# Rotary columns of the latent queries: one matrix product for both, the sine and cosine products taken from one copy

## The chip, the cores and the metric

The kernel runs on one core of one Trainium2 chip. The metric is the device time of one execution in microseconds (us); the figure for a kernel is the median of its runs. TensorE (PE) multiplies matrices, VectorE (DVE), ScalarE (ACT) and GpSimd (POOL) work on elements, and SyncE (SP) issues most of the DMAs. SBUF is the working memory of 128 partitions; PSUM takes the results of TensorE in banks of 128 x 512 floats.

## The reference, cut to what matters

A stack of two layers of a first block and one layer of a second runs over 256 tokens of 1024 features in fp32. Each of the two layers has a mixer, in which half of the heads use latent attention. Eight heads have queries of 96 features: 64 are used as they are ("nope") and 32 are rotated by the token's position. The rotated key is shared by the heads.

```python
def rope(x, positions):
    half = x.shape[-1] // 2
    ...
    x1 = x[..., :half].astype(jnp.float32)
    x2 = x[..., half:].astype(jnp.float32)
    out = jnp.concatenate([x1 * cos - x2 * sin, x2 * cos + x1 * sin], axis=-1)
...
q = (rms_norm(c_q, q_norm_g) @ w_uq).reshape(B, S, MLA_HEADS, MLA_QK_DIM)
q = jnp.concatenate([q[..., :MLA_NOPE_DIM], rope(q[..., MLA_NOPE_DIM:], positions)], axis=-1)
kv = (rms_norm(c_kv, kv_norm_g) @ w_ukv).reshape(B, S, MLA_HEADS, MLA_NOPE_DIM + MLA_V_DIM)
k_pe = rope(k_rope[:, :, None, :], positions)
k = jnp.concatenate([k_nope, k_pe], axis=-1)
o_mla = causal_block_attention(q, k, v_mla).reshape(B, S, MLA_WIDTH)
```

## The kernel before, in words

Every fp32 product is made of three TensorE matmuls (`mm3`, lines 181 to 183): weights and activations are each split into a high part and a low part (ScalarE rounds, VectorE subtracts), and high x high, high x low and low x high are added up in PSUM. The split weights lie in a ring of eight tiles `whl`, fed from a ring of four tiles `raw` that SP's DMAs fill. VectorE, ScalarE and GpSimd instructions that go through the wrappers `V`, `A` and `G` (line 134 in the profile) are given priority over the rest; apart from that, each engine has its instructions in the order that a scheduler wrote when the program was built, and works them off in that order.

`mixer` runs once per layer. It projects the tokens, normalises the latents into `cT` (transposed: features on partitions, tokens along the row), builds the rotated key in `krs`, and then runs the groups of dilated attention and after them the groups of latent attention. At the first latent group the hook `latent()` is called. It loads and splits `w_uq` and `w_ukv`, and projects:

- queries: `w_uq` has 96 columns a head. The split is stored at 128 columns a head: the 96, and after them a copy of the 32 rotary columns with their halves exchanged (the casts of lines 728 and 729). So a head fills 128 partitions of the result: 64 nope, 32 rotary, 32 rotary exchanged. Two heads go into one PSUM bank, four banks in all, one after the other in the same bank `pf1`: 18 matmuls of 256 columns each (`projB`, three k-steps, two column tiles, three matmuls). One VectorE multiplication per bank by the table `Mq` (the scale, the cosines, and the sines with their sign) empties it into `qT`.
- keys: `kT` has 128 partitions a head: 64 nope, the rotated key, and the rotated key a second time. The product of `qT` and `kT` over 128 partitions then adds the cosine part and the sine part of the rotated query.
- two banks for the nope keys and two for the values, through `pf1` too.

While a bank is emptied, TensorE does other work: transposes of the last dilated group (`tp`), and matmuls of a hook that prepares the memory's keys and values for the cross attention (`pf` from `mem_hi` and `mem_lo`); these are called fill here. After the key banks the scores (line 416, `ps` from `kT` and `qT`) begin.

`tables()` computes the angles and `Mq` in layer 0. `b2` and `ones1` belong to the second block, far later (lines 1208 and 1234).

Of the kernel before, what the change touches and what calls it, by code (L numbers as in the profile page):

```python
# [83 lines left out]
def body(nc, tc, I, out, ctx):  # L84
# [61 lines left out]
    trib = const.tile([128, 128], BF16, name="trib")  # L146
    gT1 = const.tile([128, 74], F32, name="gT1")
    gT2 = const.tile([128, 90], F32, name="gT2")
    ones1 = const.tile([1, 128], F32, name="ones1")
    small = const.tile([128, 64], F32, name="small")  # L150
    gatep = [small[:, 0:48].rearrange("p (t h b) -> p t h b", t=2, h=8)]
    rq2 = small[:, 48:64].rearrange("p (t h) -> p t h", t=2)
# [308 lines left out]
    A.activation(junk[:, 0:1], mhalf[:, 0:1], AF.Square)  # L461
    for c in range(2):
        nc.sync.dma_start(x[0][:, c * 512:c * 512 + 512], I["x"][0, 0:128, c * 512:c * 512 + 512])
    G.memset(ones1, 1.0)
    b = ps([128, 16], "pf0")
    PE.transpose(b, g0, ident[:16, :16])
    V.tensor_copy(gT1[:, 0:16], b)
# [98 lines left out]
        scale_heads(dst, src.rearrange("p (h d) -> p h d", h=nh), r, nh, hd)  # L566


    Mq = const.tile([128, T], F32, name="Mq")
    ktab = const.tile([128, 2, 64], F32, name="ktab")  # L570
    f_d = drp.tile([8, 384], F32, name="f_d")

    def tables():
        tb = sc([128, D], True)
        ta = sc([128, D], True)
        rb, oh, fs = tb[0:33, 0:8], tb[0:33, 8:392], tb[0:8, 400:784]
        G.memset(rb, 1.0)
        nc.scalar.dma_start(rb[0:32], I["rel_bias"])
        nc.scalar.dma_start(oh, I["c_bucket"])
        b = ps([8, 384], "tp")  # L580
        PE.matmul(b, rb, oh, start=True, stop=True)
        V.tensor_copy(fs, b)
        nc.scalar.dma_start(f_d, fs)
        pi, a, k = ta[:, 0:T].bitcast(I32), ta[:, T:2 * T], ta[:, 2 * T:3 * T]
        M = ta[:, 3 * T:4 * T]
        nc.scalar.dma_start(pi, I["positions"][0].partition_broadcast(128))
        V.tensor_copy(a, pi)
        V.tensor_scalar(a, a, cm[:, ROPE:ROPE + 1], None, ALU.mult)
        V.tensor_scalar(k, a, 1.0 / TWO_PI, cm[:, ROPE + 1:ROPE + 2], ALU.mult, ALU.add)
        V.tensor_scalar(k, k, MAGIC, None, ALU.add)  # L590
        V.tensor_scalar(k, k, -MAGIC, None, ALU.add)
        for c in (C1, C2, C3):
            V.scalar_tensor_tensor(a, k, -c, a, ALU.mult, ALU.add)
        V.tensor_scalar(a, a, cm[:, ROPE + 2:ROPE + 3], None, ALU.add)
        V.tensor_scalar(a, a, PI_LO, -PI_LO, ALU.min, ALU.max)
        A.activation(M, a, AF.Sin)
        V.tensor_scalar(M, M, cm[:, ROPE + 3:ROPE + 4], None, ALU.mult)
        V.tensor_scalar(Mq, M, 96.0 ** -0.5, None, ALU.mult)
        V.memset(Mq[0:64], 96.0 ** -0.5)

        def rows():
            b = ps([128, 2, 128], "tp")
            for t in range(2):
                PE.transpose(b[:, t], M[:, t * 128:t * 128 + 128], ident)
            V.tensor_copy(ktab, b[:, :, 64:128])

        return rows
# [15 lines left out]
    def mixer(l, hT, first, mid=None, hooks={}):  # L623
# [54 lines left out]
        for t in range(2):  # L678
            kr = krs[:, t]
            p1, p2 = kr[:, 128:160], kr[:, 160:192]  # L680
            V.tensor_tensor(out=p1, in0=kraw[:, t], in1=ktab[:, t, 0:32], op=ALU.mult)
            V.tensor_tensor(out=p2[:, 0:16], in0=kraw[:, t, 16:32], in1=ktab[:, t, 32:48], op=ALU.mult)
            V.tensor_tensor(out=p2[:, 16:32], in0=kraw[:, t, 0:16], in1=ktab[:, t, 48:64], op=ALU.mult)
            G.memset(kr[:, 0:64], 0.0)
            V.tensor_tensor(out=kr[:, 64:96], in0=p1, in1=p2, op=ALU.add)
            V.tensor_tensor(out=kr[:, 96:128], in0=p1, in1=p2, op=ALU.add)
        wd = load_all(w, 8, 1184, 512, gp)
        for i, b in enumerate(projB(wd, hT, 4, "ps", at={6: lambda: memory([0])} if l == 0 else {})):
            copy_any(qkd[:, 1, 2 * i:2 * i + 2], b)
# [25 lines left out]

        def latent():

            wq = []
            for k in range(3):
                raw = rawp.tile([128, 8, 96], F32, tag="raw", name="raw")  # L720
                nc.sync.dma_start(raw, I["w_uq"][l][k * 128:k * 128 + 128, :].rearrange("p (h c) -> p h c", h=8))
                hl = whlp.tile([128, 2, 8, 128], F32R, tag="whl", name="whl")
                g = GI["q_norm_g", l][k]
                nc.scalar.activation(hl[:, 0, :, 0:96], raw, AF.Copy, scale=g)
                nc.vector.scalar_tensor_tensor(hl[:, 1, :, 0:96], raw, g, hl[:, 0, :, 0:96].bitcast(F32), ALU.mult, ALU.subtract)
                for i in range(2):
                    f32v = hl[:, i].bitcast(F32)
                    nc.vector.tensor_copy(hl[:, i, :, 96:112], f32v[:, :, 80:96])
                    nc.vector.tensor_copy(hl[:, i, :, 112:128], f32v[:, :, 64:80])
                wq.append((hl[:, 0].rearrange("p h c -> p (h c)"), hl[:, 1].rearrange("p h c -> p (h c)")))  # L730
            wkv = []
            for k in range(2):
                raw = rawp.tile([128, 8, 128], F32, tag="raw", name="raw")
                nc.sync.dma_start(raw, I["w_ukv"][l][k * 128:k * 128 + 128, :].rearrange("p (h c) -> p h c", h=8))
                hl = whlp.tile([128, 2, 2, 8, 64], F32R, tag="whl", name="whl")
                g = GI["kv_norm_g", l][k]
                for j in range(2):
                    nc.scalar.activation(hl[:, 0, j], raw[:, :, j * 64:j * 64 + 64], AF.Copy, scale=g)
                    nc.vector.scalar_tensor_tensor(hl[:, 1, j], raw[:, :, j * 64:j * 64 + 64], g, hl[:, 0, j].bitcast(F32),
                                           ALU.mult, ALU.subtract)  # L740
                wkv.append([[hl[:, i, j].rearrange("p h c -> p (h c)") for i in range(2)] for j in range(2)])
            qT = s8([128, 8, T], F32, "qT")
            for i in range(4):
                b, = projB([(h_[:, i * 256:], l_[:, i * 256:]) for h_, l_ in wq], cT, 2, "pf1")
                V.tensor_tensor(out=qT[:, 2 * i:2 * i + 2], in0=b, in1=Mq.unsqueeze(1).to_broadcast([128, 2, T]),
                                op=ALU.mult)
            for i in range(2):
                b, = projB([(w_[0][0][:, i * 256:], w_[0][1][:, i * 256:]) for w_ in wkv], cT, 2, "pf1", k0=3)
                for c in range(2):
                    h = 2 * (2 * i + c)  # L750
                    copy_any(kT[0:64, h], b[0:64, c])
                    copy_any(kT[0:64, h + 1], b[64:128, c])
            cTv = (cT[0][:, 3:5], cT[1][:, 3:5])
            for t in range(2):
                b, = projA([w_[1] for w_ in wkv], cTv, t, [(0, 512)], "pf1")
                copy_any(VV[:, t, 0:512], b)
            mla["qT"] = qT
# [241 lines left out]
    def mixer2(hT, first):  # L999
# [92 lines left out]
            V.tensor_tensor(out=v, in0=v, in1=lng[:, 512:], op=ALU.add)  # L1092
        ww = load_all(w, 8, 2048, 280, gp)
        nc.sync.dma_start(w2, I["cmp_w2_2"][0].rearrange("a (k p) d -> p a k d", p=128))
        b2 = smp.tile([1, 128], F32, tag="b2", name="b2", bufs=1)
        nc.sync.dma_start(b2, I["cmp_b2_2"][0:1].rearrange("o a d -> o (a d)"))
        sw = sc([128, 8, 128], True)
        nc.sync.dma_start(sw, I["sg_w_2"][0].rearrange("g t s -> t g s"))
# [328 lines left out]
```

## Time and profile before

| | us |
|---|---|
| median of 3 runs (1206.07 to 1213.22) | 1208.72 |
| the profiled execution | 1211.78 |
| its span, first to last instruction | 1210.0 |
| TensorE busy | 1185.9 (98%) |
| VectorE busy | 780.6 (65%) |
| ScalarE busy | 706.6 (58%) |
| GpSimd busy | 83.9 (7%) |

Busy time is the union of the instructions' spans on an engine. Matmuls overlap in their pipeline, so a busy TensorE can still hold short waits; the distance between the starts of two matmuls tells what one costs. The start of layer 0 up to about 80 us is fed by DMA; the latent projection of layer 0 lies at 111 to 139 us, that of layer 1 at 516 to 544 us. TensorE's mean granted clock is 0.996 of its full 2.4 GHz.

### The profile page before, as it was taken

The numbers are of one execution on the slowest core, as the hardware profiler recorded it, in microseconds if no ns is written. First come the engines' busy times: TensorE is split into PE (matmuls) and PEld (weight loads), VectorE is DVE, ScalarE is ACT, GpSimd is POOL, SyncE is SP. The second block draws the span as 40 slices with busy tenths as digits, with TensorE's granted clock in tenths as the row PEclk, the third lists the DMA queues.
The fourth block names the chain that finished last, engine by engine and source line by source line (L and its number), as shares of the span: only waits on it lengthen the run. The fifth ranks groups of instructions, "written<-read, shape, count | busy, mean of one in ns | idle before, by whom it ended". The sixth has DMA issues, their size and how long they took to land.

```text
span 1210.0 us, 19379 instructions
## 1 busy us (share of the span) xinstructions
PE 1185.9 (98%) x7262; PEld 1029.7 (85%) x7262; DVE 780.6 (65%) x1484; ACT 706.6 (58%) x1434; POOL 83.9 (7%) x161
## 2 busy tenths in 40 slices
PE   8999999999999999999999999999999999999998
PEld 6898888889989899888888889997877787899897
DVE  6767766575565575766757665556767657656653
ACT  7765655565554575745647555556575557645541
POOL 0100010110000020000202000001022011000000
PEclk9999999999999999999999999999998999999999
DMA  8955356266656376543725756655663224665550
GB/s 261 312 181 175 96 201 245 65 229 193 187 180 195 112 263 201 163 138 123 278 88 192 238 179 200 186 178 172 194 210 105 87 88 141 209 190 191 181 187 35
DMA packets 92189, 213.23 MB, mean 176 GB/s; under 512 B 7285, under 2 KB 21055, under 8 KB 91327
## 3 DMA queue, kind: packets, MB, share of 16 engines
q1 hardware_dynamic: 91666, 211.62, 53.8%
q8 instruction: 57, 0.93, 0.3%
q10 hardware_dynamic: 428, 0.37, 0.1%
q14 instruction: 38, 0.30, 0.1%
HBM read 205.66 MB, written 6.30 MB: 175 GB/s over the span
## 4 chain that ended last, share of the span: by engine, by line
PE 77%; DMA 7%; DVE 6%; ACT 6%; issue 2%; POOL 2%; SPq 0%; ACTq 0%; POOLq 0%; DVEq 0%
PE ps L183 11%; PE ps L181 11%; PE ps L182 11%; PE pf L181 8%; PE pf L182 8%; PE pf L183 8%; PE tp L183 3%; PE tp L182 3%; PE tp L181 3%; ACT whl L173 3%; DVE whl L174 2%; PE ps L426 2%; ACT junk L134 1%; PE ps L416 1%; PE ps L827 1%
## 5 line engine op out<-in xcount | busy, mean ns | idle before, releaser
L174 DVE SCALAR_TENSOR_TENSOR whl<-raw,gT,whl 128x512 fp32r<-128x512 f32 (+5 forms) x432 | 307.6, 751 | 117.1 <-ACT whl L173 116.6
L173 ACT ACTIVATE whl<-raw,gT 128x512 fp32r<-128x512 f32 (+5 forms) x432 | 289.3, 717 | 137.6 <-issue 56.0
L170 DVE TENSOR_TENSOR whl<-raw,whl 128x512 fp32r<-128x512 f32 x264 | 170.4, 687 | 92.1 <-ACT whl L169 91.7
L169 ACT ACTIVATE whl<-raw 128x512 fp32r<-128x512 f32 x264 | 152.5, 629 | 108.0 <-issue 86.0
L181 PE MATMUL ps<-whl,mid 128*128 128x512 f32 x384 | 150.2, 391 | 0.0
L182 PE MATMUL ps<-whl,mid 128*128 128x512 f32 x384 | 149.6, 390 | 0.0
L183 PE MATMUL ps<-whl,mid 128*128 128x512 f32 x384 | 149.4, 389 | 0.0
L181 PE MATMUL pf<-hT,whl 128*128 128x256 f32 x352 | 100.0, 284 | 0.0
L182 PE MATMUL pf<-hT,whl 128*128 128x256 f32 x352 | 99.7, 283 | 0.0
L183 PE MATMUL pf<-hT,whl 128*128 128x256 f32 x352 | 99.7, 283 | 0.0
L181 PE MATMUL ps<-whl,hT 128*128 128x512 f32 (+4 forms) x240 | 85.6, 357 | 0.0
L183 PEld LDWEIGHTS ps<-whl,mid 128*128 128x128 f32 x384 | 72.1, 188 | 15.2
L183 PE MATMUL ps<-whl,hT 128*128 128x512 f32 (+4 forms) x240 | 84.1, 350 | 0.4 <-DVE hT L134 0.4
L181 PEld LDWEIGHTS ps<-whl,mid 128*128 128x128 f32 x384 | 72.2, 188 | 14.3
L182 PEld LDWEIGHTS ps<-whl,mid 128*128 128x128 f32 x384 | 72.2, 188 | 14.2
L182 PE MATMUL ps<-whl,hT 128*128 128x512 f32 (+4 forms) x240 | 84.1, 350 | 0.0
L183 PE MATMUL tp<-hT,whl 128*128 128x256 f32 x288 | 81.5, 283 | 0.0
L182 PE MATMUL tp<-hT,whl 128*128 128x256 f32 x288 | 81.5, 283 | 0.0
L181 PE MATMUL tp<-hT,whl 128*128 128x256 f32 x288 | 81.5, 283 | 0.0
L182 PEld LDWEIGHTS pf<-hT,whl 128*128 128x128 f32 x352 | 67.5, 192 | 0.3
L181 PEld LDWEIGHTS pf<-hT,whl 128*128 128x128 f32 x352 | 67.5, 192 | 0.3
L183 PEld LDWEIGHTS pf<-hT,whl 128*128 128x128 f32 x352 | 67.5, 192 | 0.0
(322 smaller groups left out, 2502.2 us busy)
## 6 DMA issues: line engine op xcount, KB each, us to landing
raw<-in_w_up_dram SPq DMA_DIRECT2D x64, 512.0 KB
raw<-in_w_down_dram SPq DMA_DIRECT2D x64, 512.0 KB
raw<-in_w_ff_dram SPq DMA_DIRECT2D x64, 512.0 KB
raw<-in_w_in_dram SPq DMA_DIRECT2D x40, 512.0 KB
raw<-in_w_xk_dram SPq DMA_DIRECT2D x16, 512.0 KB
raw<-in_w_xv_dram SPq DMA_DIRECT2D x16, 512.0 KB
raw<-in_w_mix_out_dram SPq DMA_DIRECT2D x16, 512.0 KB
raw<-in_w_xq_dram SPq DMA_DIRECT2D x16, 512.0 KB
```

Source lines behind the costliest of these rows:

```text
L134: return f(*args, **kw)
L169: nc.scalar.activation(hl[:, 0, c:d], raw[:, c:d], AF.Copy)
L170: nc.vector.tensor_tensor(out=hl[:, 1, c:d], in0=raw[:, c:d], in1=hl[:, 0, c:d].bitcast(F32), op=ALU.subtract)
L173: nc.scalar.activation(hi[:, i], r[:, i], AF.Copy, scale=g[i])
L174: nc.vector.scalar_tensor_tensor(lo[:, i], r[:, i], g[i], hi[:, i].bitcast(F32), ALU.mult, ALU.subtract)
L181: PE.matmul(o, sh, mh, start=start, stop=False, skip_group_check=True)
L182: PE.matmul(o, sh, ml, start=False, stop=False, skip_group_check=True)
L183: PE.matmul(o, sl, mh, start=False, stop=stop, skip_group_check=True)
L416: PE.matmul(s[:, i], qf(h[i], tq), kf(h[i], nk), start=i == 0 and bias is not None, stop=True, skip_group_check=True)
L426: PE.matmul(cell["o"][j * 64:j * 64 + 64, h // 2], vf(h, kb), pp[j][i][kb] if bias is None else pp[j][i][kb][:, ::-1], start=begin and i = ...
L827: PE.matmul(s[:, i], qT[:, c, tq], kT[:, c], start=(i == 0 and k == 0), stop=k == nkt - 1, skip_group_check=True)
```

## The change

The rotary columns are multiplied once. The split of `w_uq` is stored as 256 rotary columns (8 heads x 32) followed by 512 nope columns, without copies, so that the queries need six column tiles in three banks. The first bank holds the rotary columns of all heads, four heads in a column tile. ScalarE copies it to SBUF (`rope`), and from the copy VectorE makes the four products with the cosines (into partitions 64 to 95 of `qT`) and GpSimd the four with the sines (into 96 to 127). The two nope banks are emptied in halves, one by ScalarE and one by VectorE. The exchange of halves moves to the key: its second copy is built exchanged. The table `Mq` becomes `csq`, with the 32 rows of cosines and sines repeated for the four groups of partitions. For space, `b2` and `ones1` now lie in `csq` and `ktab`, and are filled once these are no longer read.

```diff
@@ tables
-        V.tensor_scalar(Mq, M, 96.0 ** -0.5, None, ALU.mult)
-        V.memset(Mq[0:64], 96.0 ** -0.5)
+        for g in range(4):
+            nc.vector.tensor_scalar(csq[32 * g:32 * g + 32, 0], M[64:96], 96.0 ** -0.5, None, ALU.mult)
+            nc.scalar.activation(csq[32 * g:32 * g + 32, 1], M[96:128], AF.Copy, scale=-(96.0 ** -0.5))
@@ mixer, the rotated key
-            V.tensor_tensor(out=kr[:, 96:128], in0=p1, in1=p2, op=ALU.add)
+            V.tensor_tensor(out=kr[:, 96:112], in0=p1[:, 16:32], in1=p2[:, 16:32], op=ALU.add)
+            V.tensor_tensor(out=kr[:, 112:128], in0=p1[:, 0:16], in1=p2[:, 0:16], op=ALU.add)
@@ latent, the split of w_uq
-                hl = whlp.tile([128, 2, 8, 128], F32R, tag="whl", name="whl")
+                hl = whlp.tile([128, 2, 768], F32R, tag="whl", name="whl")
                 g = GI["q_norm_g", l][k]
-                nc.scalar.activation(hl[:, 0, :, 0:96], raw, AF.Copy, scale=g)
-                nc.vector.scalar_tensor_tensor(hl[:, 1, :, 0:96], raw, g, hl[:, 0, :, 0:96].bitcast(F32), ALU.mult, ALU.subtract)
-                for i in range(2):
-                    f32v = hl[:, i].bitcast(F32)
-                    nc.vector.tensor_copy(hl[:, i, :, 96:112], f32v[:, :, 80:96])
-                    nc.vector.tensor_copy(hl[:, i, :, 112:128], f32v[:, :, 64:80])
...
+                for c0, n, o in ((64, 32, 0), (0, 64, 256)):
+                    hi, lo = (hl[:, i, o:o + 8 * n].rearrange("p (h c) -> p h c", h=8) for i in range(2))
+                    nc.scalar.activation(hi, raw[:, :, c0:c0 + n], AF.Copy, scale=g)
+                    nc.vector.scalar_tensor_tensor(lo, raw[:, :, c0:c0 + n], g, hi.bitcast(F32), ALU.mult, ALU.subtract)
@@ latent, the query banks
-            for i in range(4):
+            for i in range(3):
                 b, = projB([(h_[:, i * 256:], l_[:, i * 256:]) for h_, l_ in wq], cT, 2, "pf1")
-                V.tensor_tensor(out=qT[:, 2 * i:2 * i + 2], in0=b, in1=Mq.unsqueeze(1).to_broadcast([128, 2, T]),
-                                op=ALU.mult)
+                if i == 0:
+                    rope = sc([128, 2, T])
+                    A.activation(rope, b, AF.Copy)
+                    for g in range(4):
+                        pr = slice(32 * g, 32 * g + 32)
+                        for j, eng in enumerate((V, G)):
+                            eng.tensor_tensor(out=qT[64 + 32 * j:96 + 32 * j, g:8:4], in0=rope[pr],
+                                              in1=csq[pr, j].unsqueeze(1).to_broadcast([32, 2, T]), op=ALU.mult)
+                else:
+                    h = 4 * (i - 1)
+                    A.activation(qT[0:64, h:h + 4:2], b[0:64], AF.Copy, scale=96.0 ** -0.5)
+                    V.tensor_scalar(qT[0:64, h + 1:h + 4:2], b[64:128], 96.0 ** -0.5, None, ALU.mult)
@@ the second block
-        b2 = smp.tile([1, 128], F32, tag="b2", name="b2", bufs=1)
+        b2 = csq[0:1, 0, 0:128]
+        ones1 = ktab[0:1].rearrange("p t c -> p (t c)")
+        G.memset(ones1, 1.0)
         nc.sync.dma_start(b2, I["cmp_b2_2"][0:1].rearrange("o a d -> o (a d)"))
```

The first place where the order of instructions moves is VectorE in `latent()` of layer 0; `pf` with a number is one query or key bank, `e` are probabilities of the last dilated groups. Before:

```order
L134 TENSOR_TENSOR qT<-pf_1379,Mq 128x512 [waits PE_49]
L134 TENSOR_SCALAR e<-e,den 128x256 [waits DVE_49]
L134 TENSOR_SCALAR e<-e,den 128x256
L134 TENSOR_TENSOR qT<-pf_1399,Mq 128x512 [waits PE_49]
L134 TENSOR_TENSOR qT<-pf_1419,Mq 128x512 [waits PE_49]
L174 SCALAR_TENSOR_TENSOR whl<-raw,gT_95,whl 128x512 [waits DMAHW5_49,Activation_49]
L174 SCALAR_TENSOR_TENSOR whl<-raw,gT_95,whl 128x512 [waits Activation_49]
L134 TENSOR_TENSOR qT<-pf_1439,Mq 128x512 [waits PE_49]
```

and with the change:

```order
L134 TENSOR_SCALAR e<-e,den 128x256 [waits DVE_49]
L134 TENSOR_SCALAR e<-e,den 128x256
L134 TENSOR_TENSOR qT<-sc,csq 32x2x256 [waits Activation_49]
L134 TENSOR_TENSOR qT<-sc,csq 32x2x256 x3
L134 TENSOR_SCALAR qT<-pf_1408 64x2x256 [waits Activation_49]
L173 SCALAR_TENSOR_TENSOR whl<-raw,gT_95,whl 128x512 [waits DMAHW4_49,Activation_49]
L173 SCALAR_TENSOR_TENSOR whl<-raw,gT_95,whl 128x512 [waits Activation_49]
L169 TENSOR_TENSOR whl<-raw,whl 128x512 [waits DMAHW5_49,Activation_49]
L134 TENSOR_SCALAR qT<-pf_1429 64x2x256 [waits Activation_49]
```

VectorE's half of the second bank (`pf_1408`) now stands behind the four cosine products and waits for ScalarE's half. On GpSimd the four sine products stand alone, with nothing near them.

The second place is TensorE at the first scores of layer 0. Before:

```order
L416 MATMUL ps<-kT,qT 128x128 [waits Activation_49]
L416 MATMUL ps<-kT,qT 128x256
L416 MATMUL ps<-kT,qT 128x128 [waits DVE_49]
L182 MATMUL pf_1724<-whl,mem_hi 128x512
L416 MATMUL ps<-kT,qT 128x128 [waits Activation_49]
```

and with the change (lines of helpers are one lower):

```order
L415 MATMUL ps<-kT,qT 128x128 [waits Activation_49,Pool_49]
L415 MATMUL ps<-kT,qT 128x256
L415 MATMUL ps<-kT,qT 128x128 [waits DVE_49,Pool_49]
L415 MATMUL ps<-kT,qT 128x128 [waits Activation_49]
L415 MATMUL ps<-kT,qT 128x256
```

The scores wait for GpSimd now. Ahead of them stand 16 fill matmuls between the banks, as before, and 18 query matmuls fewer.

The third place is SP's queue in the start of layer 0, where the loads of the last weights of the first projection (`w_in`), of the bias table (`H`, through `f_d`), of the memory and of its key weights (`w_xk`) follow each other. Before:

```order
L163 DMA raw_697<-in_w_in_dram 128x2x512 [waits DMAHW4_49,DMAHW2_49,DVE_49]
L614 DMA H_511<-f_d_130 128x8x256 [waits DMAHW1_49]
L163 DMA raw_835<-in_w_xk_dram 128x2x512 [waits DMAHW5_49,DVE_49]
L163 DMA raw_842<-in_w_xk_dram 128x2x512 [waits DMAHW6_49,DVE_49,Activation_49]
L489 DMA sc_641<-in_mem_dram 128x1024 [waits PE_49]
L700 DMA b_d_131<-H_511 128x2048 [waits DMAHW7_49,DMAHW3_49]
L489 DMA sc_652<-in_mem_dram 128x1024 [waits DMAHW0_49,PE_49]
```

and with the change:

```order
L614 DMA H_515<-f_d_128 128x8x256 [waits DMAHW7_49]
L162 DMA raw_703<-in_w_in_dram 128x2x512 [waits DMAHW3_49,DVE_49]
L162 DMA raw_841<-in_w_xk_dram 128x2x512 [waits DMAHW4_49,DVE_49]
L487 DMA sc_645<-in_mem_dram 128x1024 [waits PE_49]
L701 DMA b_d_129<-H_515 128x2048 [waits DMAHW5_49,DMAHW1_49]
L162 DMA raw_848<-in_w_xk_dram 128x2x512 [waits DMAHW6_49,DVE_49,Activation_49]
L487 DMA sc_656<-in_mem_dram 128x1024 [waits PE_49]
```

The bias table goes ahead of the last weights, and the second load of key weights goes behind the first half of the memory and the store `b_d`.

## Rows read from the trace of the kernel before

**Rows 1.** The page: span, and busy time of each engine
```profile
span 1210.0 us, 19379 instructions
...
PE 1185.9 (98%) x7262; PEld 1029.7 (85%) x7262; DVE 780.6 (65%) x1484; ACT 706.6 (58%) x1434; POOL 83.9 (7%) x161
```

**Rows 2.** Timeline of TensorE, layer 0: start us, us, what
```profile
116.24 0.39 PE L181 MATMUL pf<-cT,whl 128*128 128x256 f32 x1
...
119.50 0.31 PE L181 MATMUL pf<-cT,whl 128*128 128x256 f32 x1
...
122.63 0.38 PE L181 MATMUL pf<-cT,whl 128*128 128x256 f32 x1
...
124.88 0.39 PE L181 MATMUL pf<-whl,mem_hi 128*128 128x512 f32 x1
...
128.70 1.12 PE L416 MATMUL ps<-kT,qT 128*128 128x128 f32 x6
```

**Rows 3.** The same timeline, layer 1: first matmul of the fourth bank, and what follows
```profile
527.75 0.38 PE L181 MATMUL pf<-cT,whl 128*128 128x256 f32 x1
...
530.00 0.39 PE L181 MATMUL pf<-whl,mem_hi 128*128 128x512 f32 x1
```

**Rows 4.** Waits, 111 to 135 us: us in total, times, longest
```profile
PEld pf L181 <- DVE qT L134: 0.7, 3, 0.3
```

**Rows 5.** Groups of VectorE by shape, whole run: busy us, mean ns | idle before
```profile
L134 DVE TENSOR_TENSOR qT<-pf,Mq 128x512 f32<-128x512 f32 x8 | 5.5, 691 | 9.4 <-PE pf L183 9.4
...
L729 DVE CAST whl<-whl 128x128 fp32r<-128x128 f32 x12 | 2.7, 224 | 0.0
```

**Rows 6.** Groups of ScalarE by shape, whole run
```profile
L134 ACT ACTIVATE kT<-pf 64x256 f32<-64x256 f32 x8 | 3.0, 378 | 9.7 <-PE pf L183 7.2 <-DVE kT L134 2.4
...
L134 ACT ACTIVATE VV<-pf 128x512 f32<-128x512 f32 x4 | 2.4, 594 | 0.3 <-PE pf L183 0.3
...
L134 ACT ACTIVATE scf<-scf 128x256 f32<-128x256 f32 x1 | 0.4, 417 | 0.0
```

**Rows 7.** Timeline of VectorE, layer 0
```profile
115.49 0.69 DVE L134 TENSOR_TENSOR qT<-pf,Mq 128x512 f32<-128x512 f32 x1 [0.21 <-PE pf L183]
...
124.40 1.41 DVE L174 SCALAR_TENSOR_TENSOR whl<-raw,gT,whl 128x512 fp32r<-128x512 f32 x2 [1.82 <-ACT whl L173]
...
126.33 2.49 DVE L170 TENSOR_TENSOR whl<-raw,whl 128x512 fp32r<-128x512 f32 x4
```

**Rows 8.** Groups of GpSimd by shape, whole run
```profile
L134 POOL TENSOR_TENSOR small<-small,mhalf 128x8 f32<-128x8 f32 x2 | 3.3, 1638 | 0.2
...
L134 POOL TENSOR_TENSOR lv<-lv 128x4 f32<-128x4 f32 x2 | 0.4, 200 | 0.2
```

**Rows 9.** Timeline of VectorE and GpSimd, 245 to 249 us
```profile
245.45 2.07 DVE L174 SCALAR_TENSOR_TENSOR whl<-raw,gT,whl 128x512 fp32r<-128x512 f32 x3
247.44 0.69 DVE L134 TENSOR_TENSOR relu<-relu 128x512 f32<-128x512 f32 x1
...
246.35 1.86 POOL L134 TENSOR_SCALAR lv<-sm 128x1 f32<-128x1 f32 x1 [2.93 <-ACT junk L134]
```

**Rows 10.** Timeline of VectorE and GpSimd, 757 to 760 us
```profile
758.28 2.32 DVE L174 SCALAR_TENSOR_TENSOR whl<-raw,gT,whl 128x512 fp32r<-128x512 f32 x2 [1.04 <-ACT whl L173]
...
758.30 1.10 POOL L134 TENSOR_SCALAR_AFFINE_SELECT scf<-scf 128x1024 f32<-128x1024 f32 x1 [95.30 <-DMA scf<-in_sg_w_dram]
```

**Rows 11.** Windows: stretch, length, busy of PE, PEld, DVE, ACT, POOL, clock, DMA
```profile
140.00:150.00 10.00, 10.00 (x75) 8.14 (x75) 10.00 (x26) 8.70 (x27) 0.00 (x0) 1.00 0.33 105
```

**Rows 12.** Start of layer 0: timeline of ScalarE and TensorE
```profile
50.68 2.73 ACT L173 ACTIVATE whl<-raw,gT 128x512 fp32r<-128x512 f32 x4 [4.04 <-DMA raw<-in_w_xk_dram]
...
54.67 0.44 PE L604 MATMUL tp<-cm,scf 128*128 128x128 f32 x2 [1.69 <-DVE cT L134]
```

**Rows 13.** Start of layer 0: the chain that ended last
```profile
49.77 7.30 DMA sc<-in_mem_dram
```

**Rows 14.** Timeline of SP's queue, layer 1, 530 to 532 us
```profile
530.96 0.33 SPq L163 DMA_DIRECT2D raw<-in_w_mix_out_dram  x1
```

More of the change, by code (lines that the diff above doesn't have):

```diff
@@ L148, in body @@
     gT2 = const.tile([128, 90], F32, name="gT2")
-    ones1 = const.tile([1, 128], F32, name="ones1")
     small = const.tile([128, 64], F32, name="small")
@@ L463, in body @@
         nc.sync.dma_start(x[0][:, c * 512:c * 512 + 512], I["x"][0, 0:128, c * 512:c * 512 + 512])
-    G.memset(ones1, 1.0)
     b = ps([128, 16], "pf0")
@@ L566, in head_norm @@
         scale_heads(dst, src.rearrange("p (h d) -> p h d", h=nh), r, nh, hd)
-    Mq = const.tile([128, T], F32, name="Mq")
+    csq = const.tile([128, 2, T], F32, name="csq")
     ktab = const.tile([128, 2, 64], F32, name="ktab")
@@ L721, in latent @@
                 nc.sync.dma_start(raw, I["w_uq"][l][k * 128:k * 128 + 128, :].rearrange("p (h c) -> p h c", h=8))
-                hl = whlp.tile([128, 2, 8, 128], F32R, tag="whl", name="whl")
+                hl = whlp.tile([128, 2, 768], F32R, tag="whl", name="whl")
                 g = GI["q_norm_g", l][k]
-                nc.scalar.activation(hl[:, 0, :, 0:96], raw, AF.Copy, scale=g)
-                nc.vector.scalar_tensor_tensor(hl[:, 1, :, 0:96], raw, g, hl[:, 0, :, 0:96].bitcast(F32), ALU.mult, ALU.subtract)
-                for i in range(2):
-                    f32v = hl[:, i].bitcast(F32)
-                    nc.vector.tensor_copy(hl[:, i, :, 96:112], f32v[:, :, 80:96])
-                    nc.vector.tensor_copy(hl[:, i, :, 112:128], f32v[:, :, 64:80])
-                wq.append((hl[:, 0].rearrange("p h c -> p (h c)"), hl[:, 1].rearrange("p h c -> p (h c)")))
+                for c0, n, o in ((64, 32, 0), (0, 64, 256)):
+                    hi, lo = (hl[:, i, o:o + 8 * n].rearrange("p (h c) -> p h c", h=8) for i in range(2))
+                    nc.scalar.activation(hi, raw[:, :, c0:c0 + n], AF.Copy, scale=g)
+                    nc.vector.scalar_tensor_tensor(lo, raw[:, :, c0:c0 + n], g, hi.bitcast(F32), ALU.mult, ALU.subtract)
+                wq.append((hl[:, 0], hl[:, 1]))
             wkv = []
```

## The prediction

> **What bounds the kernel.** I read the page first: TensorE is busy for 1185.9 of 1210.0 us, VectorE for 780.6 [rows 1]. That makes TensorE the suspect, but busy spans overlap, so the timeline of the stretch has to say what a matmul costs and whether it waits. In layer 0 the four query banks, the two key banks and the fill between them follow each other from 116.24 to 128.70 us [rows 2], where the scores begin. The waits of this stretch come next: TensorE stood still for VectorE's emptying of a query bank for 0.7 us over three turns [rows 4]. So the stretch is TensorE's own work with small waits, and work taken out of it should be time gained, unless a turn between two banks gets longer. After it, in 140 to 150 us, VectorE is busy all 10 us and ScalarE 8.70 [rows 11]; there the softmax of the latent groups is near a second limit, which has to be weighed below.
>
> **What is removed.** The fourth query bank: 18 matmuls a layer. Its first matmul starts at 122.63 and the fill behind it at 124.88 [rows 2], so it costs 2.25 us; in layer 1 527.75 to 530.00, 2.25 us too [rows 3]. Two layers: 4.50 us. This is exact as far as TensorE goes. The casts of the exchanged columns (24 in all, some 0.22 us each [rows 5]) and the `Mq` products go from VectorE; as TensorE does not wait for them beyond the 0.7 us, I count nothing for them.
>
> **What is added, bank by bank** (layer 0, clock of the trace before).
>
> First bank, complete when VectorE starts on it at 115.49 [rows 7]. VectorE needed 0.69 us, TensorE restarted at 116.24. ScalarE's copy of such a bank takes 0.59 us [rows 6] and ScalarE has nothing else then, so the copy ends at about 116.1 and the second bank can start as before. Two of the four transposes that covered this turn now stand behind the second bank, so I allow 0.1 us.
>
> Second bank: 116.2 plus 2.2 gives 118.4. It is emptied in two halves, VectorE's waiting for ScalarE's. A half has all 512 columns on 64 partitions. The rows bound it from below by the 256-column copy on 64 partitions, 0.38 us, and from above by the whole bank, 0.59 us on ScalarE [rows 6] and 0.69 us on VectorE [rows 5]; the cost goes with columns (0.38 to 0.59 from 256 to 512), so I take 0.59 and 0.69, 1.3 us in turn, and with the handover the bank is free at 119.8. TensorE meanwhile has other work: before, from 116.24 plus 2.25, 118.49, to the third bank at 119.50 [rows 2], 1.0 us of four transposes, a mask matmul and two fill matmuls; now two transposes and one fill matmul more. A query matmul of 256 columns costs 2.25 / 18 = 0.125 us, so by columns these are an estimate of 0.25 and twice 0.06 us. It comes to the third bank at 119.8. No wait, or 0.1 us, if VectorE is free at 119.1. It has the four cosine products first. Four products with two SBUF inputs and 512 columns took 2.49 us back to back [rows 7]: 116.1 to 118.6. Free in time, with half a microsecond to spare.
>
> GpSimd makes the four sine products, and no row shows such an operation there. Below: the 128x1024 select with one input took 1.10 us [rows 10], so 512 columns cannot be much under 0.55 us. Above: twice that for the second input and as much again, 2.2 us. A multiplication of four columns takes 0.20 us, against 1.64 us for a power over eight [rows 8]: multiplications are not in the class of the power. I take 1.1 us, the two-input reading of the select, 4.4 us for four. A sentence from the Trainium skill, page GPSIMD Engine Reference, section 3.1, on an addition of 2048 columns at 4497 ns: a quarter is an estimate of 1.12 us, and the sum would be the same.
>
> **Do the two collide?** Rows 9 and 10 show they can. A one-column GpSimd instruction that takes 0.2 to 0.3 us when undisturbed stood from 246.35 to 248.21, until just after VectorE's run of three weight splits and a square had ended at 248.13 [rows 9]: GpSimd got no turn between four VectorE instructions. The other way round, two weight splits took 2.32 us beside the 1.10 us select [rows 10], where two take 1.41 us [rows 7]: VectorE stood for 0.9 us. The rule behind it is in the Trainium skill, page SBUF, section Who interferes with whom: a VectorE instruction with two SBUF inputs and a GpSimd instruction that reads SBUF take a port pair from each other for a whole instruction, and who issues first decides. Both rows agree with it, and it speaks against this change, which starts both kinds of product on the same event. With VectorE first, as rows 9 suggest for a run, VectorE is not delayed, and GpSimd runs from 118.6 to 123.0. With one GpSimd product first, VectorE is done at 119.7, its half at 120.4, and TensorE waits for 0.5 us. I take 0.15 us a layer.
>
> Third bank: its halves come behind two or three weight splits on either engine. Ten fill matmuls of 512 columns, an estimate of 2.5 us, cover them; two splits of 1.41 us together [rows 7], a third, and VectorE's half (0.69) sum to 2.7, so 0.1 us a layer, between 0 and 0.5.
>
> Scores: they began at 128.70, now at about 126.5. All sine products are there at 123.0: 3.5 us of cover. If that cover is gone, each product costs its own length.
>
> The softmax behind it: VectorE has full use in 140 to 150 us [rows 11], but its work there starts with the scores, and these come earlier by as much, so the gain passes through.
>
> Other edits. The weight split in two pieces costs a start more per k-step and engine: 0.59 less twice the 0.21 us between 0.59 and 0.38 [rows 6] is 0.17 us, three times a layer, beside fill; without cover 0.5 us a layer on either engine, less than the casts that VectorE loses there. `csq` costs four ScalarE instructions of at most 0.42 us [rows 6], 1.7 us at about 47 us, where ScalarE stood for 4.04 us for a DMA [rows 12]. The rotated key has one VectorE instruction more for each half of the tokens, of 16 columns; each lies between 0 and the 0.22 us of a 128-column cast [rows 5], beside the projection of the dilated keys: 0, and 0.9 us in all if that cover is gone. `b2`'s load now waits in SP's queue in layer 1 for the cosine products, ahead of the third output weight; that was not issued before 530.96 [rows 14], while the first bank is emptied well before the fourth began at 527.75 [rows 3], so nothing is late.
>
> The start: SP's queue moves. TensorE stood for 1.69 us there, for VectorE's and ScalarE's `cT` work that stands behind four weight splits [rows 12]. The chain there runs through the second half of the memory (7.30 us) [rows 13]. The same bytes go through full DMA engines before that half, so I take 0; at best the 1.69 us goes, at worst one more load of that kind stands ahead, also some 1.7 us.
>
> **Sum.** 4.50 minus 0.35 a layer (0.1, 0.15, 0.1), that is 0.7, and 0 for the start: 3.8 us less. The span goes from 1210.0 to 1206.2, the profiled execution from 1211.8 to 1208.0; the median shown, 1208.7, lies 3.1 below that execution and goes to 1204.9. This is 0.3%, and 0.5% (6.0 us) is about what a measurement of this kernel tells from no change.
>
> **Rivals.**
> - The port goes the other way: GpSimd keeps it for all four sine products, or one in between each cosine product. Then VectorE is done at 123.0 or 121.9, its half at 123.7 or 122.6, and TensorE waits 3.8 or 2.7 us a layer. For it: rows 10. Against it: rows 9, where the engine with a run of short instructions kept the port, and that is VectorE. Time: 1208.7 - 3.8 + 7.6 = 1212.5, or 1210.3. Chance 0.15.
> - The softmax absorbs it: the latent groups end when VectorE and ScalarE are done, not TensorE. For it: the full 10 us in rows 11. Against it: the earlier scores. Up to 2 us a layer lost, 1206.5 to 1208.9. Chance 0.12.
> - The start gains its 1.69 us and more, since a wait there is DMA order: 1201 to 1202.7. Chance 0.12.
> - Slower: a sine product costs far more than a row shows. From 118.6 the scores of 126.5 leave 7.9 us, 2 us each; beyond that the scores stand. At 3.3 us each they stand 5.3 us a layer: 1208.7 - 3.8 + 10.6 = 1215.5. It decides from 3.2 us on. For it: the power over eight columns [rows 8]. Against it: the four-column multiplication. Chance 0.07.
> - My forecast, 1203 to 1206.5: 0.54.
>
> **Range.** 1200.5 (4.5 less, the start's 1.7, and 2 us of spread of the runs) to 1211 (the port by turns). It leaves out the slow rival, half of the port's and some spread. Faster by over 0.5% (under 1202.7): most of the start's case and a little of mine, 0.18. Slower by over 0.5% (above 1214.8): 0.08. Within: 0.74.
>
> **What would show it.** TensorE with 36 matmuls of `cT` by 256 columns fewer; scores of layer 0 about 2 us earlier against the start of the second bank. Cosine products in one run of 2.5 us and sine products after them, or in between. If TensorE's wait ahead of the third bank is over 1 us a layer, the port is the cause; if the scores wait for GpSimd, its price; if the shift is there at the scores and gone at the output projection, the softmax. A different time at 76 us, when the start is over, is the start's.

## The result and the profile after

The changed kernel takes 1216.2 us (median of 9 runs), the kernel before 1210.0 in runs beside them: ratio 1.0054, 95% interval 1.004 to 1.0068. By the ratio it is slower by 6.5 us, where the prediction had it 3.8 us faster, and lies outside the range. The page of the changed kernel:

```profile
span 1214.9 us, 19324 instructions
...
PE 1181.6 (97%) x7226; PEld 1025.9 (84%) x7226; DVE 789.6 (65%) x1476; ACT 712.9 (59%) x1450; POOL 98.1 (8%) x169
```

Against [rows 1] TensorE has lost its 36 matmuls and 4.3 us of busy time, and yet the profiled span is 4.9 us longer. So TensorE waits somewhere. The list of waits of layer 0's latent stretch, 111 to 135 us (us in total, times, longest), answers to [rows 4]:

```profile
PE pf L180 <- DVE qT L134: 2.6, 1, 2.6
```

The 0.7 us over three turns are now one wait of 2.6 us, for VectorE's emptying of a query bank; layer 1 has the same. It is the sign that the prediction named for the port, a wait of over 1 us ahead of the third bank. TensorE's timeline of layer 0, which answers to [rows 2], shows where (first matmul of the first, second and third bank, and the scores):

```profile
112.58 0.36 PE L180 MATMUL pf<-cT,whl 128*128 128x256 f32 x1
...
117.29 0.39 PE L180 MATMUL pf<-cT,whl 128*128 128x256 f32 x1
...
123.78 0.58 PE L180 MATMUL pf<-cT,whl 128*128 128x256 f32 x1 [2.62 <-DVE qT L134]
...
131.76 1.77 PE L415 MATMUL ps<-kT,qT 128*128 128x128 f32 x10
```

TensorE has its fill done at 121.16 and stands until 123.78. Every VectorE instruction of that wait, taken one at a time from the timeline, and GpSimd's beside them:

```profile
117.27 0.68 DVE L134 TENSOR_TENSOR qT<-sc,csq 32x512 f32<-32x512 f32 x1 [0.18 <-ACT sc L134]
117.97 1.68 DVE L134 TENSOR_TENSOR qT<-sc,csq 32x512 f32<-32x512 f32 x1
119.66 1.66 DVE L134 TENSOR_TENSOR qT<-sc,csq 32x512 f32<-32x512 f32 x1
121.34 1.66 DVE L134 TENSOR_TENSOR qT<-sc,csq 32x512 f32<-32x512 f32 x1
123.03 0.69 DVE L134 TENSOR_SCALAR qT<-pf 64x512 f32<-64x512 f32 x1
...
117.37 1.74 POOL L134 TENSOR_TENSOR qT<-sc,csq 32x512 f32<-32x512 f32 x1 [56.74 <-ACT sc L134]
119.18 1.60 POOL L134 TENSOR_TENSOR qT<-sc,csq 32x512 f32<-32x512 f32 x1
120.84 1.61 POOL L134 TENSOR_TENSOR qT<-sc,csq 32x512 f32<-32x512 f32 x1
122.53 1.60 POOL L134 TENSOR_TENSOR qT<-sc,csq 32x512 f32<-32x512 f32 x1
```

The two engines take strict turns. VectorE comes first, by 0.10 us, and is delayed all the same from its second product on. VectorE's first cosine product takes 0.68 us; each of the other three takes 1.66 to 1.68, because a sine product goes ahead of it. Four take 5.7 us instead of the 2.5 of the prediction, and VectorE's half of the second bank, queued behind them, is ready at 123.72. TensorE pays once more, as its clock falls here before the wait ends (granted 0.90 over the wait). The windows show layer 0's wait, the 2.7 us behind it, and the same two stretches of layer 1 (stretch, length, TensorE's busy time, granted clock, DMA share, GB/s):

```profile
121.16:123.78 2.62, 0.01 (x2) 0.90 0.00 0
123.78:126.50 2.72, 2.72 (x12) 0.50 0.00 0
...
527.90:530.50 2.60, 0.02 (x1) 1.00 0.00 0
530.50:533.20 2.70, 2.67 (x20) 1.00 0.03 6
```

Behind the wait of layer 0 the granted clock is 0.50, the 1.2 GHz level: 12 matmuls in the time that 20 take in layer 1, where the same wait left the clock at 2.4 GHz.

### The profile page after: what moved, and what is told of

Same layout as the page of the kernel before. It is cut to its first block, busy times and chain, and to the rows that moved or that the text cites. A ratio compares the mean times of both kernels' runs of the same rounds, so it can differ in the third digit from the quotient of the medians.

```text
span 1214.9 us, 19324 instructions
## 1 busy us (share of the span) xinstructions
PE 1181.6 (97%) x7226; PEld 1025.9 (84%) x7226; DVE 789.6 (65%) x1476; ACT 712.9 (59%) x1450; POOL 98.1 (8%) x169
## 4 chain that ended last, share of the span: by engine, by line
PE 75%; DVE 8%; DMA 7%; ACT 5%; issue 2%; POOL 1%; SPq 0%; ACTq 0%; POOLq 0%; DVEq 0%
PE ps L180 11%; PE ps L181 11%; PE ps L182 11%; PE pf L180 8%; PE pf L181 8%; PE pf L182 8%; PE tp L182 3%; PE tp L181 3%; PE tp L180 3%; DVE whl L173 3%; ACT whl L172 2%; DMA raw<-in_w_in_dram 2%; PE ps L425 2%; ACT junk L134 1%; PE ps L837 1%
```

## The experiments

Theory A: the loss is in the latent stretches, where the two engines' products take turns and VectorE's half comes late. Rival B: the loss is in the changed order of loads, at the start and in the last block. Rival C: GpSimd's price is on the path of the scores. Two measures from TensorE's timeline go beside each ratio, as single spans differ by several us for reasons outside these stretches: the time of layer 0's first query matmul (what the start costs), and each layer's time from its first query matmul to the first score matmul of its cross-attention (what the latent groups cost). Layer 0 of the kernel before, and the end of the same stretch in the changed kernel:

```profile
111.28 0.36 PE L181 MATMUL pf<-cT,whl 128*128 128x256 f32 x1
...
193.36 0.81 PE L827 MATMUL ps<-xkT,qT 128*128 128x256 f32 x3
...
196.30 1.02 PE L837 MATMUL ps<-xkT,qT 128*128 128x256 f32 x4
```

| kernel | ratio to before, 95% | first query matmul | layer 0 | layer 1 |
|---|---|---|---|---|
| before | 1 | 111.28 | 82.08 | 81.99 |
| after | 1.0054, 1.004 to 1.0068 | 112.58 | 83.72 | 82.50 |
| after, once more (E9) | 1.0054, 1.0039 to 1.007 | 111.92 | 82.50 | 83.97 |
| E1 halves on ScalarE | 0.9994, 0.9981 to 1.0008 | 112.13 | 80.54 | 80.52 |
| E2 products on VectorE | 1.0013, 0.9999 to 1.0027 | 112.12 | 82.10 | 82.15 |
| E3 products on GpSimd | 1.0045, 1.0029 to 1.0062 | 112.32 | 84.26 | 82.83 |
| E4 before, row of ones moved | 1.0012, 1.0 to 1.0024 | 113.30 | 81.97 | 81.99 |
| E5 VectorE first | 1.0018, 1.0004 to 1.0031 | 111.24 | 81.95 | 81.92 |
| E6 = E1 and E2 | 0.9981, 0.9967 to 0.9995 | 112.52 | 80.17 | 80.18 |
| E7 = E6, start restored | 0.9968, 0.9954 to 0.9981 | 110.43 | 80.20 | 80.15 |
| E8 after, start restored | 1.0029, 1.0015 to 1.0042 | 110.79 | 83.98 | 83.94 |
| E10 cosine from PSUM | 1.0033, 1.0019 to 1.0046 | 112.08 | 82.51 | 82.50 |
| E11 sine in pieces | one run | 112.05 | 80.85 | 80.81 |
| E12 one-column instructions | one run | 110.83 | 80.17 | 80.20 |

**E1: both halves of a bank on ScalarE.**

```diff
-                    V.tensor_scalar(qT[0:64, h + 1:h + 4:2], b[64:128], 96.0 ** -0.5, None, ALU.mult)
+                    A.activation(qT[0:64, h + 1:h + 4:2], b[64:128], AF.Copy, scale=96.0 ** -0.5)
```

> The changed kernel, with both halves of the second and third query bank emptied by ScalarE, so that VectorE's half no longer stands behind the cosine products. Theory A (the two engines take turns at the products, and VectorE's half comes too late for TensorE): the cosine products still take 5.7 us and the sine products 6.75 us, but TensorE's waits of 2.6 us ahead of the third bank go in both layers, and the low clock after the one in layer 0 with them; first query matmul to scores 15.5 us in layer 0 instead of 19.2; about 6 us less than the changed kernel, a ratio of 1.000 to the kernel before. Rival B (the loss comes from the changed order of loads at the start and in the last block, the latent stretch pays for itself): the ratio stays near 1.005. Rival C (what GpSimd's products cost is on the path of the scores): the wait moves to the scores, ratio 1.003 to 1.005.

Timelines of VectorE, GpSimd and ScalarE, layer 0:

```profile
116.83 5.76 DVE L134 TENSOR_TENSOR qT<-sc,csq 32x512 f32<-32x512 f32 x4 [0.18 <-ACT sc L134]
...
116.92 6.83 POOL L134 TENSOR_TENSOR qT<-sc,csq 32x512 f32<-32x512 f32 x4 [56.95 <-ACT sc L134]
...
119.31 1.20 ACT L134 ACTIVATE qT<-pf 64x512 f32<-64x512 f32 x2 [2.51 <-PE pf L182]
```

The turns stay as they were (5.76 and 6.83 us); only what stood behind them is elsewhere. TensorE's wait of 2.6 us is gone, and the ratio falls from 1.0054 to 0.9994, 7.3 us. The two layers hold 5.3 us of that (161.1 us in E1, 166.2 and 166.5 in the two profiles of the changed kernel); the rest is no more than the intervals. Theory A holds, and rival C falls: the sine products end as late as before and nothing waits for them.

**E2 and E3: all products on one engine.**

```diff
-                        for j, eng in enumerate((V, G)):
+                        for j, eng in enumerate((V, V)):
```

E3 has (G, G) in that place.

> The changed kernel with all eight products on VectorE, none on GpSimd. Theory A: an undisturbed product takes 0.62 us, so that VectorE alone does all eight in 5.0 us, less than the 6.75 us that the two engines took for them together; its half of the second bank is done 0.7 us earlier, the wait ahead of the third bank is 1.9 us instead of 2.6, ratio 1.003 to 1.005. Were the 1.4 us of a cosine product VectorE's own price in this shape (32 partitions to 32 others), eight would take 11.5 us, the wait would be over 8 us a layer, ratio 1.013.

> The changed kernel with all eight products on GpSimd, none on VectorE. It gives GpSimd's own price. Theory A: a product takes clearly less than the 1.69 us that it took in turn with VectorE's, about 1.1 us, eight are done at about 126.3 us in layer 0, and the scores hardly wait; the wait ahead of the third bank is gone; ratio 1.000. If 1.69 us is GpSimd's own price: eight end at 131 us, the scores wait 4 us a layer, ratio 1.004.

E2, VectorE's timeline; then E3, GpSimd and VectorE one at a time, and TensorE:

```profile
116.82 5.58 DVE L134 TENSOR_TENSOR qT<-sc,csq 32x512 f32<-32x512 f32 x8 [0.19 <-ACT sc L134]
```

```profile
119.80 1.28 POOL L134 TENSOR_TENSOR qT<-sc,csq 32x512 f32<-32x512 f32 x1
120.12 0.69 DVE L134 TENSOR_SCALAR qT<-pf 64x512 f32<-64x512 f32 x1 [3.29 <-ACT qT L134]
...
122.64 1.69 DVE L173 SCALAR_TENSOR_TENSOR whl<-raw,gT,whl 128x512 fp32r<-128x512 f32 x1 [1.83 <-ACT whl L172]
123.84 1.63 POOL L134 TENSOR_TENSOR qT<-sc,csq 32x512 f32<-32x512 f32 x1
...
128.35 0.58 PE L180 MATMUL pf<-cT,whl 128*128 128x256 f32 x1 [2.74 <-DVE qT L134]
```

VectorE alone makes eight products in 5.58 us, less than the 6.75 us in which both engines made four each. TensorE's wait ahead of the third bank is only 0.37 us in E2, as twelve fill matmuls stand there in its order instead of three, and the ratio is better than expected; but these are missing later, where TensorE waits 0.24 and 0.55 us for ScalarE at the key and value banks, and a layer is still 1.9 us longer than in E6. The waits are 1.1 us of that; the rest is TensorE's busy time and is not explained. A sine product costs GpSimd 1.28 us by itself and 1.60 in turn. E3 went the other way than expected: the wait did not go, it moved. GpSimd's run now meets VectorE's weight splits, which take 1.69 us instead of 0.7 (two in 1.41 us, [rows 7]), and TensorE waits 2.74 us for the half of the third bank behind them. VectorE's half itself, with PSUM as its input, took 0.69 us in the middle of a sine product (120.12).

**E4, E8 and E9: the start.** In the change GpSimd's writing of a row of ones goes from the start to the last block. E4 makes that move, and that of the bias row, in the kernel before (first diff); E8 writes such a row at its old place in the changed kernel (second diff; into the key table's first row, which is overwritten later):

```diff
-    ones1 = const.tile([1, 128], F32, name="ones1")
...
-    G.memset(ones1, 1.0)
...
-        b2 = smp.tile([1, 128], F32, tag="b2", name="b2", bufs=1)
+        b2 = Mq[0:1, 0:128]
+        ones1 = ktab[0:1].rearrange("p t c -> p (t c)")
+        G.memset(ones1, 1.0)
```

```diff
+    ktab = const.tile([128, 2, 64], F32, name="ktab")
...
+    G.memset(ktab[0:1], 1.0)
     b = ps([128, 16], "pf0")
     PE.transpose(b, g0, ident[:16, :16])
...
-    ktab = const.tile([128, 2, 64], F32, name="ktab")
```

> The kernel before, with one edit of the change alone: the row of ones and the bias row of the last block have no place of their own but use that of the query factors and of the key table, and are written in the last block. The order of SP's loads at the start is then that of the changed kernel. Rival B: the first query matmul of layer 0 is 1.2 us later, and the output weight of the last block comes late, ratio 1.002 to 1.004. Theory A alone: ratio 1.000, within 0.001.

> The changed kernel with that one row written at the start again, nothing else undone. If the start's order costs 0.85 to 1.5 us: first query matmul at 111.3 us instead of 112.6, ratio 1.004 to 1.0045 where the changed kernel has 1.0054. The 2.6 us waits ahead of the third bank stay.

> The changed kernel as it is, in the same manner as the experiments, so that its ratio and theirs stand beside each other: 1.0054 again, within its interval (1.004 to 1.0068); waits of 2.6 us ahead of the third bank in both layers; first query matmul of layer 0 between 112.0 and 113.3 us.

E4 alone costs 1.5 us (0 to 2.9), E8 gives back 3.0 us (1.0029 beside 1.0054), more than was expected of it; its waits of 2.6 us stay. A third pair, E7 beside E6, gives 1.6 us. With the row at the start SP's queue has these loads in the order of before, without it in that of after; the ten profiles with the new order have the first query matmul at 112.2 us on average (111.2 to 113.3), the four with the old at 110.8 (110.4 to 111.3), 1.4 us apart. E4's profile, the latest of the ten, also has TensorE at the 1.2 GHz level from 56.87 to 60.28 us, which no other has. So part of B is right: the start costs 1.5 to 3 us. More of the loss is A's: 7.3 us in E1, 5.3 of it in the two layers. A cost of the last block is not shown: from layer 1's cross-attention to the end of the span it takes 611.5 us before, 613.1 and 611.8 in the changed kernel, 611.9 in E4 and 610.2 in E6, which loads the bias row as the changed kernel does.

**E5: VectorE first.** The order on which the prediction was built: the loops over engines and groups change places, and GpSimd's products wait for a one-column copy that VectorE makes behind its own four.

```diff
-                    for g in range(4):
-                        pr = slice(32 * g, 32 * g + 32)
-                        for j, eng in enumerate((V, G)):
+                    for j, eng in enumerate((V, G)):
+                        for g in range(4):
+                            pr = slice(32 * g, 32 * g + 32)
...
+                        if j == 0:
+                            V.tensor_copy(rope[:, 0, 0:1], rope[:, 0, 0:1])
```

> The changed kernel, with GpSimd's sine products held back until VectorE's four cosine products are done (a one-column copy of the rope tile by VectorE behind them). This is the order that the prediction took for granted. If the wrong order at the port was the whole error: the cosine products take 2.8 us (4 x 0.70), VectorE's half of the second bank is done 3 us earlier, no wait ahead of the third bank, and the ratio comes down to 0.998 to 1.000. If the products were bound to collide with something (theory A in its wider form: any VectorE instruction on two SBUF inputs waits while GpSimd multiplies): the sine products run from 120.1 to 126 us, VectorE's weight splits of 0.7 us take 1.7 us beside them, its half of the third bank is late and TensorE waits ahead of the key bank instead, 1 to 2.7 us a layer; ratio 1.003 to 1.005.

Timelines of VectorE, GpSimd and TensorE:

```profile
115.94 2.78 DVE L134 TENSOR_TENSOR qT<-sc,csq 32x512 f32<-32x512 f32 x4 [0.19 <-ACT sc L134]
119.04 0.69 DVE L134 TENSOR_SCALAR qT<-pf 64x512 f32<-64x512 f32 x1
121.57 2.45 DVE L173 SCALAR_TENSOR_TENSOR whl<-raw,gT,whl 128x512 fp32r<-128x512 f32 x2 [1.83 <-ACT whl L172]
123.94 1.76 DVE L169 TENSOR_TENSOR whl<-raw,whl 128x512 fp32r<-128x512 f32 x1
...
119.08 6.08 POOL L134 TENSOR_TENSOR qT<-sc,csq 32x512 f32<-32x512 f32 x4 [59.76 <-ACT qT L134]
...
126.36 0.38 PE L180 MATMUL pf<-cT,whl 128*128 128x256 f32 x1 [1.83 <-DVE qT L134]
```

The wait ahead of the third bank is gone, and one of 1.83 us stands ahead of the key bank: three splits stretch from 2.1 to 4.1 us beside the sine products. Even with the order that it assumed, the predicted time would have been too low (1.0018): the change gives 0.1 us a layer instead of 1.9.

**E10, E11 and E12: what the turn is.** E10 lets VectorE read the bank in PSUM, so that the factors are its only SBUF input; E11 is E1 with each sine product cut in two; E12 is E7 with six one-column additions on GpSimd beside VectorE's run. The diffs of the three:

```diff
-                            eng.tensor_tensor(out=qT[64 + 32 * j:96 + 32 * j, g:8:4], in0=rope[pr],
+                            eng.tensor_tensor(out=qT[64 + 32 * j:96 + 32 * j, g:8:4], in0=(b if eng is V else rope)[pr],
```

```diff
-                            eng.tensor_tensor(out=qT[64 + 32 * j:96 + 32 * j, g:8:4], in0=rope[pr],
-                                              in1=csq[pr, j].unsqueeze(1).to_broadcast([32, 2, T]), op=ALU.mult)
+                            for hh in ((slice(0, 2),) if eng is V else (slice(0, 1), slice(1, 2))):
+                                eng.tensor_tensor(out=qT[64 + 32 * j:96 + 32 * j, g + 4 * hh.start:g + 4 * hh.stop - 3:4], in0=rope[pr, hh],
+                                                  in1=csq[pr, j].unsqueeze(1).to_broadcast([32, hh.stop - hh.start, T]), op=ALU.mult)
```

```diff
+                    one = smp.tile([128, 8], F32, tag="lv", name="lv", bufs=6)
+                    for c in range(6):
+                        G.tensor_scalar(one[:, c:c + 1], rope[:, 0, c:c + 1], rope[:, 1, c:c + 1], EPS, ALU.add, ALU.add)
```

> The changed kernel with VectorE's cosine products reading the first bank straight from PSUM, with the factors as their only SBUF input; GpSimd's read the copy as before. If the turn is one between instructions on two SBUF inputs: each cosine product takes 0.68 us beside GpSimd's, 2.8 us for four; a sine product takes 1.28 us undisturbed, not 1.60; the first bank comes free 2.2 us later, and what TensorE has of other work covers part of it. If any VectorE instruction that reads SBUF takes turns with GpSimd: 5.7 us again, and the bank is held for all of it. Ratio, with the weight splits colliding with the sine products later in either case: 1.002 to 1.005.

> The first experiment's kernel (both halves on ScalarE) with each sine product cut into two of 256 columns. If VectorE waits for a whole GpSimd instruction: a cosine product in turn takes 1.2 us instead of 1.68, four 4.2 us instead of 5.7. If GpSimd takes the port in smaller steps than an instruction: 1.68 us and 5.7 us stay.

> The kernel with all eight products on VectorE, halves on ScalarE and the start's row restored, and six additions of one column each on GpSimd, which become ready with the rope copy (extra work that nothing reads). It repeats the situation on which the prediction rested: one-column GpSimd instructions against a run of VectorE instructions on two SBUF inputs. If VectorE keeps the port through a run: the first of the six lasts until the run's end, over 5 us, and the rest come after it. If turns change at each instruction: each of the six takes between one and three VectorE instructions, 0.7 to 2.1 us, the first two or more are done while VectorE's run goes on, and the run is hardly longer than 5.6 us, as a turn of one column is short.

VectorE and GpSimd of E10, of E11 and of E12:

```profile
116.78 2.79 DVE L134 TENSOR_TENSOR qT<-pf,csq 32x512 f32<-32x512 f32 x4 [0.19 <-ACT sc L134]
...
116.88 5.35 POOL L134 TENSOR_TENSOR qT<-sc,csq 32x512 f32<-32x512 f32 x4 [56.81 <-ACT sc L134]
```

```profile
116.74 4.11 DVE L134 TENSOR_TENSOR qT<-sc,csq 32x512 f32<-32x512 f32 x4 [0.18 <-ACT sc L134]
...
118.10 1.06 POOL L134 TENSOR_TENSOR qT<-sc,csq 32x256 f32<-32x256 f32 x1
```

```profile
115.53 5.59 DVE L134 TENSOR_TENSOR qT<-sc,csq 32x512 f32<-32x512 f32 x8 [0.18 <-ACT sc L134]
...
115.59 4.27 POOL L134 TENSOR_SCALAR lv<-sc 128x1 f32<-128x1 f32 x6 [56.50 <-ACT sc L134]
```

E10: with one SBUF input neither engine feels the other (2.79 us for four, 5.35 for four); but the bank is held longer, and the second bank starts 7.64 us after the first query matmul instead of 4.71. The fill that covers this is missing later, where TensorE waits 0.56, 0.24 and 0.55 us for ScalarE at the key and value banks, so the time is not won (1.0033). E11: with pieces of half the length four cosine products take 4.11 us, so what VectorE waits for is one GpSimd instruction. E12: six one-column instructions get a turn each while VectorE's run goes on, done at 119.86 where the run ends at 121.12, and the run is no longer for it.

**E6 and E7: the change without both costs.** E6 joins the edits of E1 and E2; E7 adds E8's row.

> The changed kernel with all eight products on VectorE and both halves of the second and third query bank on ScalarE: neither GpSimd nor the turn of the port is left, and nothing of a query bank stands behind the products. Theory A: eight products in 5.6 us, weight splits at their own 0.7 us, first query matmul to scores 14.8 us, no wait ahead of a bank over 0.3 us; ratio 0.998 to 1.000, as with ScalarE's halves alone. A rival (VectorE itself is now too full, and the latent groups end late): the gain at the scores is given back by the output projection, ratio 1.002.

> The kernel of the run before in this list, with GpSimd's writing of a row of ones put back at its old place at the start (into the key table's row, which is overwritten later); the order of SP's loads at the start is then that of the kernel before. If the start's order costs 0.85 to 1.5 us: the first query matmul of layer 0 is at 111.3 us again instead of 112.1, and the ratio is 0.001 lower than without it, 0.997 to 0.999. If the profiles' start differs by chance: no difference.

E7's VectorE and ScalarE, layer 0:

```profile
115.13 5.59 DVE L134 TENSOR_TENSOR qT<-sc,csq 32x512 f32<-32x512 f32 x8 [0.18 <-ACT sc L134]
120.75 1.42 DVE L174 SCALAR_TENSOR_TENSOR whl<-raw,gT,whl 128x512 fp32r<-128x512 f32 x2
...
117.60 1.20 ACT L134 ACTIVATE qT<-pf 64x512 f32<-64x512 f32 x2 [2.50 <-PE pf L183]
```

GpSimd has no product, the splits have their own 1.42 us again, and TensorE's longest wait for a query bank is 0.12 us. E6 has 0.9981, E7 0.9968: 3.9 us less than before (2.3 to 5.6), the lowest ratio of these kernels, though its interval overlaps that of E6.

## Why the prediction was wrong

**The fourth bank, 4.50 us: right in kind, too large.** In E6 and E7 a layer is 1.8 to 1.9 us shorter than before, which is the prediction's 2.25 less 0.35, but not by its terms. Over both layers TensorE's busy time falls from 163.2 to 159.3 us, 3.9 instead of 4.50, and its waits grow from 0.9 to 1.1 us, 0.2 instead of 0.7. The two errors cancel. E7 comes nearest to the kernel that the sum described, with the old start and no product that waits for GpSimd, but its products are all on VectorE and its halves all on ScalarE; that its 3.9 us are the predicted 3.8 is in part luck. The key exchange and the split in two pieces were not run by themselves. The rival of the softmax falls, as the gain is there at the cross-attention.

**The port: the step that failed.** It was "With VectorE first, as rows 9 suggest for a run, VectorE is not delayed", priced at 0.15 us a layer. The wait is 2.6 us a layer. Two layers without the low clock behind it (after, layer 1; E9, layer 0) are 2.3 us longer than in E6 (82.50 against 80.17). VectorE was first, as the step assumed, but it kept the port for one instruction and not for its run. The step made a rule of one instruction in [rows 9], which had lost its turn inside a run. The same trace had a counterexample that was not looked for, timeline of VectorE and GpSimd, 1026 to 1030 us of the kernel before:

```profile
1026.01 4.06 DVE L174 SCALAR_TENSOR_TENSOR whl<-raw,gT,whl 128x512 fp32r<-128x512 f32 x6
...
1027.26 0.91 POOL L134 TENSOR_SCALAR lv<-sm 128x1 f32<-128x1 f32 x1 [5.40 <-ACT junk L134]
1028.25 0.93 POOL L134 TENSOR_TENSOR lv<-lv,mhalf 128x1 f32<-128x1 f32 x1
```

Here two GpSimd instructions end inside one VectorE run of six splits, and E12 shows it as the usual case. The one in [rows 9] began at 246.35, inside the second of the three splits, so it was passed over at two changes of instruction and not at each of three between four. Why it was passed over stays open. The first rival had the mechanism, "one in between each cosine product", and its wait (2.7 us) to 0.1; it got a chance of 0.15, and its price of 1210.3 lacked the clock and the start.

**The clock: missing.** Nothing in the prediction priced what TensorE's clock does after such a wait. Of the six waits of 2.6 us in after, E9 and E8, four are followed by a granted clock at the 1.2 GHz level for a stretch; those layers are 1.2 to 1.5 us longer than the other two (83.72 to 83.98 against 82.50). E3's two waits of 2.74 us are split in the same way (84.26 and 82.83).

**The start: 0, measured at 1.5 to 3 us.** "The same bytes go through full DMA engines before that half" looked at the load that was taken out of the queue, and not at what had put the queue in order; its worst case, 1.7 us, is about what came. The edit that mattered is a memset of one row on GpSimd: E8 writes one there and has the old order and the old time back. `b2`'s own load was issued at 524.72 us and held nothing up, as predicted.

**GpSimd's price: in its bounds, without effect alone.** 1.28 us by itself, 1.1 taken. The scores wait for no sine product in any run, so the rival that ended slower was wrong in its mechanism; that its time of 1215.5 came close is luck.

**Splits against sine products: not priced.** The third bank's 0.1 us took splits at their own length. In the changed kernel the sine products end before the splits begin, so it does not show; in E3 and E5 it costs 2.74 and 1.83 us.

**The sum by what was measured**, for the two layers: -3.7 (E6, E7) plus twice 2.3 for the wait, plus 1.4 for the low clock in four of six layers, that is 1.9, plus 1.5 to 3 for the start: 4.3 to 5.8 us, against 6.5 with an interval of 4.8 to 8.2. The first three terms are differences of layer times, so they add up to what the layers show; only the start is measured apart from them. What is left, 0.7 to 2.2 us, no run explains; the interval reaches 1.7 us to either side.

## What to carry to other kernels

Sharing these products between VectorE and GpSimd, each with two SBUF operands, speeds up nothing: eight took 5.6 us on VectorE and 6.75 us on both. What counts is not the products but what is queued behind them on VectorE: a short emptying of a PSUM bank that TensorE needs belongs on an engine outside that contest (7.3 us here, 5.3 of it seen in the two layers). Moving it ahead of the products was not run. And where a scheduler decides the order, an edit far from the change, such as a row of ones that is written elsewhere, is compared in every queue before it is priced at nothing.

## What the runs showed of the hardware

The turn between VectorE and GpSimd is by instruction and alternates: 0.68 us of a VectorE product became 1.68 beside GpSimd products of 512 columns and 1.11 to 1.13 beside those of 256. The Trainium skill, page SBUF — State Buffer, section Who interferes with whom, says that who issues first keeps the shared pair for a whole instruction, and that a VectorE instruction with at most one SBUF input, outside its two-port modes, stands apart from this. E10 agrees with the second (2.79 us for four, undisturbed). For two runs side by side "first" does not settle it: the engine that waits gets the next turn, in the changed kernel at each of VectorE's products but the first. The instruction of [rows 9] is the one exception in the stretches read here.

TensorE's granted clock fell to the 1.2 GHz level with four of six equal waits of 2.6 us and held at 2.4 GHz with the other two: in layer 0 of one profile it fell and not in layer 1, and the other way round in the next profile of the same kernel. It fell with one of E3's two waits of 2.74 us and with neither of E5's two of 1.83 us. A wait of 2.6 us therefore costs a layer either 2.3 or 3.5 to 3.8 us here, against E6.
